# Residuals that lie in the output and are added onto by transfers, and last products by column halves, at the end of a diffusion trunk layer

## The chip, the cores and the metric

One core of a Trainium2 chip. The metric is the device time of one execution in microseconds (us). A profiled execution gives the trace; its times count from the start of its span.

## What is computed

One trunk layer for 128 context tokens and 512 latent tokens, 1024 wide: a mixer of attention and a gated convolution, then a feed-forward part, each normalised and added back with a gate.

```
mo, k, v = mixer(u, p, rope_tabs, ctx_k, ctx_v)
h = h + g1 * rms_norm(mo, p["g_post1"])
u = rms_norm(h, p["g_pre2"]) * (1 + sc2) + sh2
h = h + g2 * rms_norm(conv_ffn(u, p), p["g_post2"])

def conv_ffn(u, p):
    up = dwconv3(u @ p["w_up"], p["conv_ffn"])
    g, val = jnp.split(up, 2, axis=-1)
    return (jax.nn.silu(g) * val) @ p["w_down"]
```

The change concerns the last line of the layer: the product with w_down (2816 x 1024), the root of its mean square, the gain g_post2 * gate, and the addition of h, the residual of the mixer's half.

## The kernel before

The 640 tokens are five tiles of 128, t = 0 (context) and 1 to 4 (latent). The matrices are float32, and each product is made of three: high by high, high by low, low by high part (`mm3`, lines 235 to 237 of the trace's program).

**The stage of w_o** (near 617 to 645 us). For each tile `residual(t)` makes h on VectorE (DVE) in a buffer WR, and SyncE (SP) stores it to a scratch in HBM, hd[t] (line 1732). The normalised h goes on into w_up.

**The stage of w_down** (from about 940 us on). The activations come back from HBM in pairs of 128 rows. The first 512 output columns of every tile are finished near 1000 us: `first_half(t, pm)` squares them on ScalarE (ACT) with a running sum, multiplies them by the gains on DVE into EX[:, t, 0:512], adds the epsilon, and has SP load hd[t] into HX[:, t, :] (line 2341). EX holds five tiles of 1024 columns; it is what is stored in the end.

The last 512 columns follow. For the latent tiles the 2 x 2 blocks of tokens and columns are put together from seven products, `part(p, n)`, with sums on DVE in the buffers RAWS and A. The context tile has plain products, `context(p)`, into a PSUM bank pms[0]: for each pair p two k-steps of three products of 512 columns. The order of the work is the order in which the code is written; the three last pairs (`held`) are ordered so that the blocks finish one after another: tiles 3 and 4 first, then 1 and 2, then the context tile, whose 18 products are TensorE's last work.

What happens to a tile when its block is complete:
- `second_half(t, src)` (from line 2346): ACT squares the second 512 columns with a running sum. For latent tiles POOL adds both sums (line 2355) and raises the result to the power -1/2 (line 2356). For the context tile ACT takes a square root (2352) and DVE a reciprocal (2353), and DVE multiplies the PSUM bank by the gains (2351).
- `scaled2(t, x)` (line 2361): DVE multiplies the second halves of two tiles by the gains into EX.
- `stored(t, n)` (lines 2366 to 2369): in n pieces, DVE makes EX * root + HX, and SP stores the piece to the rows `yrows(t)` of the output. Tile 3 goes in one piece, the others in halves.

```
    def stored(t, n=1):
        r = ssqs[:, t, 1:2]
        for i in range(n):
            cs = slice(i * D // n, (i + 1) * D // n)
            V.scalar_tensor_tensor(out=EX[:, t, cs], in0=EX[:, t, cs], scalar=r, in1=room["h"][:, t, cs], op0=ALU.mult, op1=ALU.add)
            nc.sync.dma_start(yrows(t)[:, cs], EX[:, t, cs])
```

Each engine works through its own queue in order; waits are on counters of the other engines and of the DMA queues. SP issues every transfer of this stretch, in the order of the code. `ssqs[:, t, :]` holds the running sums and then the root of tile t. At the very end SP waits for the landing of all transfers and the engines meet in a barrier (line 2521).

Of the kernel before, what the change touches and what calls it, by code (L numbers as in the profile page):

```python
# [12 lines left out]
F32 = mybir.dt.float32  # L13
# [4 lines left out]
AF = mybir.ActivationFunctionType  # L18
ALU = mybir.AluOpType
# [6 lines left out]
NT = 5  # L26
# [8 lines left out]
NACT = NCOL - 2  # L35
PARTS = (((0, 128, 1), (128, 320, 130)), ((0, 320, 322),))
NRING = 4
FLAG = 3
DLAG = 4
EPS = 1e-6  # L40
O_K, O_V, O_B, O_C, O_X, O_GA, O_GC = 1024, 1280, 1536, 2560, 3584, 4608, 5632
# [71 lines left out]
def trunk_layer(ctx, tc, x_prompt, x_sample, cache_k, cache_v, c, c_ctx, w_ada, b_ada, g_pre1, g_post1, g_pre2,  # L113
                g_post2, w_in, q_norm, k_norm, w_att_out, conv_w, w_conv_out, w_o, w_up, conv_ffn, w_down, rope,
                y_prompt, y_sample, new_k, new_v):
    nc = tc.nc
    V, S, G, PE = nc.vector, nc.scalar, nc.gpsimd, nc.tensor
# [10 lines left out]
    def yrows(t):  # L128
        return y_prompt if t == 0 else y_sample[(t - 1) * 128:t * 128, :]
# [18 lines left out]
    def region(pool, tag, shape, dtype, name):  # L148
        return pool.tile([128] + shape, dtype, tag=tag, name=name)
# [20 lines left out]
    def ps1():  # L170
        turn[1] += 1
        return psa.tile([128, 512], F32, tag=f"s1{turn[1] % 2}", name=nm("s1"), bufs=1)
# [7 lines left out]
    state = {"next": 0, "raw": [], "cut": [], "limit": 10}  # L180
# [77 lines left out]
    mhalf = const.tile([128, 8], F32, name="mhalf")  # L258
# [13 lines left out]
    hd = dp.tile([NT, 128, D], F32, name="hd")  # L272
# [101 lines left out]
    with tc.tile_pool(name="pro", bufs=2) as pro, tc.manual_schedule(engines={mybir.EngineType.SP}):  # L374
# [258 lines left out]
        for f in range(2, KT):  # L633
# [32 lines left out]
            if f == KT - 3:  # L666
                V.tensor_scalar(out=gains[0], in0=gains[0], scalar1=HD ** -0.5, scalar2=None, op0=ALU.mult)
                for i in range(2):
                    for a in range(2):
                        V.tensor_tensor(out=tabs[i][:, :, 0, a * 32:a * 32 + 32], in0=rt[:, :, 0, a * 32:a * 32 + 32],  # L670
                                        in1=gains[i][:, :, a * 32:a * 32 + 32].broadcast_to((128, 4, 32)), op=ALU.mult)
                        for hf in range(2):
                            d0, s0 = a * 32 + hf * 16, a * 32 + (1 - hf) * 16
                            V.tensor_tensor(out=tabs[i][:, :, 1, d0:d0 + 16], in0=rt[:, :, 1, d0:d0 + 16],
                                            in1=gains[i][:, :, s0:s0 + 16].broadcast_to((128, 4, 16)), op=ALU.mult)
            if f == KT - 2:
                cut_upto(9)
                p = ps1()
# [11 lines left out]
    AH = Halves(NTOK, F32R, "AH")  # L690
    AL = region(ra, "r3", [KT, NTOK], F32R, "AL")
# [55 lines left out]
    with tc.tile_pool(name="att", bufs=1) as at:  # L747
# [11 lines left out]
        ssqs = at.tile([128, 4, 4], F32, name="ssqs")  # L759
# [13 lines left out]
        held = {}  # L773
# [126 lines left out]
        for t in range(NT):  # L900
# [30 lines left out]
            h = work(f"k{t} hi", "ACT", k_hi, [tk], [pk])  # L931
# [121 lines left out]
        for n, (g, t, pi) in enumerate(steps):  # L1053
# [52 lines left out]
            else:  # L1106
                pts[n], exs = [], []
                for h in hs:
# [16 lines left out]
                    if h:  # L1125
# [3 lines left out]
                                                                                   accum_out=mk[:, 4 + h:5 + h]), [mx], [ar[h]] + [er] * way)  # L1129
# [43 lines left out]
            if pi in (None, 1):  # L1173
                u = vcol[:, 2 * g + (t > 0):2 * g + (t > 0) + 1]
# [19 lines left out]
                r = work(f"R{n}", "ACT", spread, list(pvs), [pvr, xr])  # L1194
                o = work(f"O{n}", "DVE", whole, [r], [pvr, xr])
                a = work(f"AH{n}", "ACT", ah, [o], [pvr])
# [45 lines left out]
    sm_ = ctx.enter_context(tc.tile_pool(name="sm", bufs=2))  # L1242
# [11 lines left out]
    cut, raws, pair, TT = {}, {}, {}, {}  # L1254
# [474 lines left out]
    def residual(t):  # L1729
        h = WR[:, 2 + t % 3, :]  # L1730
        V.scalar_tensor_tensor(out=h, in0=TX[:, 2 + t % 2, :], scalar=roots[t], in1=h, op0=ALU.mult, op1=ALU.add)
        nc.sync.dma_start(hd[t], h)

    def sq_h(t):
        S.activation(TX[:, 4, :], WR[:, 2 + t % 3, :], AF.Square, accum_out=ssq[t][:, 2:3])
# [32 lines left out]
    room = {}  # L1768
# [115 lines left out]
    def wd_step(pm, t, act, w, start, stop):  # L1884
        c0 = 0 if t == 0 else 1 + t * 128
        mm3(pm, act[0][:, c0:c0 + 128], act[1][:, c0:c0 + 128], *w, start, stop)
# [16 lines left out]
    def second_gate(j):  # L1903
        i = j - DLAG
        accs = [[room["c+"], room["s"][:, 4, :]], [room["raw"][:, 4, :]]]
# [7 lines left out]
    def second_gate_load(j):  # L1913
        i = j - DLAG
        if i == 2 * KT:
# [6 lines left out]
    def strassen(j):  # L1922

        f, nxt = j - FLAG, j + 1 if j + 1 < NJ else None
        g = NJ - FLAG if nxt is None else None
        cg, cv = crows(j)
# [54 lines left out]
        if nxt:  # L1981
# [54 lines left out]
    for q in range(4):  # L2036
# [11 lines left out]
        elif q == 1:  # L2048
            half_load(0)
            p = bank(6)  # L2050
# [18 lines left out]
        for t in range(NT):  # L2069
# [5 lines left out]
            if q == 3 and t == 2:  # L2075
                p = bank(7)
# [142 lines left out]
    NPAIR, NP0 = NJ // 2 - 2, 1  # L2219
    A0 = region(ra, "r0", [4, 2 * NACT], F32R, "A0")  # L2220
    A1 = region(ra, "r1", [4, 2 * NACT], F32R, "A1")
    AL, AH = [A0[:, i, :] for i in range(3)], [A0[:, 3, :], A1[:, 0, :], A1[:, 1, :]]
# [3 lines left out]
    EX = region(rb, "r4", [NT, D], F32, "EX")  # L2226
    GJ = rb.tile([128, 2560], F32, tag="r5a", name="GJ")
    G2, JK = GJ[:, 0:2048].rearrange("p (r c) -> p r c", r=2), GJ[:, 2048:2560]
    RAWS = rb.tile([128, 2560], F32, tag="r5b", name="RAWS")
    SR, TR, C22 = RAWS[:, 0:1024], RAWS[:, 1024:2048], RAWS[:, 2048:2560]  # L2230
    SS, TS = {}, {2: T2}
    ssqs = sm_.tile([128, NT, 2], F32, name="ssqs", bufs=1)

    def s_room(p):
        i = p % 3
# [93 lines left out]
    def context(p):  # L2329
        u = state["cut"][base + p]  # L2330
        for k in range(2):
            a = [x[p % 3][:, k * NACT:(k + 1) * NACT] for x in (AH, AL)]
            wd_step(pms[0], 0, a, u.at(k), False, p == NPAIR - 1 and k == 1)

    def first_half(t, pm):
        row = 1 if t == 0 else 0
        first = ssqs[:, t, 0:1]
        S.activation(JK, pm, AF.Square, accum_out=first)
        V.tensor_tensor(out=EX[:, t, 0:512], in0=pm, in1=G2[:, row, 0:512], op=ALU.mult)
        V.tensor_scalar(out=first, in0=first, scalar1=D * EPS, scalar2=None, op0=ALU.add)  # L2340
        nc.sync.dma_start(room["h"][:, t, :], hd[t])

    def halves_of(x):
        return x.rearrange("p (i c) -> p i c", i=2)

    def second_half(t, src):
        row = 1 if t == 0 else 0
        first, second = ssqs[:, t, 0:1], ssqs[:, t, 1:2]
        S.activation(halves_of(JK), src, AF.Square, accum_out=second)  # L2349
        if t == 0:  # L2350
            V.tensor_tensor(out=EX[:, t, 512:1024], in0=pms[0], in1=G2[:, row, 512:1024], op=ALU.mult)
            S.activation(second, second, AF.Sqrt, bias=first)
            V.reciprocal(second, second)
        else:
            G.tensor_tensor(out=second, in0=second, in1=first, op=ALU.add)  # L2355
            G.tensor_tensor(out=second, in0=second, in1=mhalf[:, 0:1], op=ALU.pow)

    def scaled2(t, x):
        for i in range(2):
# [3 lines left out]

    def stored(t, n=1):
        r = ssqs[:, t, 1:2]
        for i in range(n):
            cs = slice(i * D // n, (i + 1) * D // n)
            V.scalar_tensor_tensor(out=EX[:, t, cs], in0=EX[:, t, cs], scalar=r, in1=room["h"][:, t, cs], op0=ALU.mult, op1=ALU.add)
            nc.sync.dma_start(yrows(t)[:, cs], EX[:, t, cs])


    pms = [bank(b) for b in RING if b not in BANKS[NJ - 1]] + [bank(BANKS[NJ - 1][1])]
# [19 lines left out]
    w, x, y = NJ - 3, NJ - 2, NJ - 1  # L2392
# [30 lines left out]
    base = state["next"]  # L2423
# [34 lines left out]
    held = range(NPAIR - HELD, NPAIR)  # L2458
# [20 lines left out]
    for p in held:  # L2479
        part(p, 2)  # L2480
    V.tensor_tensor(out=C1[:, 0, :], in0=accs[2], in1=p1, op=ALU.add)
    stored(3)
    for p in held:
        part(p, 3)
    V.tensor_tensor(out=C1[:, 1, :], in0=accs[3], in1=u4, op=ALU.add)
    for t in (1, 2):
        second_half(t, C1[:, :, (t - 1) * 256:t * 256])
    scaled2(1, C1)
    for p in held:
        context(p)  # L2490
    for t in (4, 1, 2):
        stored(t, 2)
    second_half(0, halves_of(pms[0]))
    stored(0, 2)
    fixed.close()

# [28 lines left out]
```

## Time and profile before

| what | value |
|---|---|
| median of 3 runs | 1074.96 us (1074.27 to 1075.36) |
| profiled execution, its own time | 1074.79 us |
| its span (first to last instruction) | 1073.0 us |
| granted TensorE clock | 0.999 |
| busy: PE / DVE / ACT / POOL | 1056.8 / 899.9 / 598.4 / 133.1 us |
| read from and written to HBM | 123.31 MB / 17.36 MB |

The span is 1.8 us shorter than the execution's own time. PE is TensorE's products, PEld its weight loads, SPq the queue of SP. A line such as L2368 is a line of the program before. In rows of the timeline the first number is the start, the second the length; in square brackets stands the idle time before it and what ended it.

### The profile page before, as it was taken

What the parts mean: (1) busy time and instruction counts of PE and PEld (TensorE: products, weight loads), DVE (VectorE), ACT (ScalarE), POOL (GpSimd) and SP (SyncE); (2) the same over time, 40 slices, a digit from 0 to 9 for tenths busy, and PEclk for the clock granted to TensorE, in tenths of its full rate; (3) what the DMA queues carried; (4) which work ended last, traced back from release to release, by engine and by line L of the source; (5) the groups of instructions that cost most, each with busy time, mean ns of one, the idle gap of its engine ahead of it and who ended that gap; (6) DMA issues with size and microseconds to landing.
All of it is one profiled execution on the core that took longest, in us unless ns stands there. A gap on an engine that the chain in (4) does not pass through costs nothing.

```text
span 1073.0 us, 20652 instructions
## 1 busy us (share of the span) xinstructions
PE 1056.8 (98%) x8216; PEld 995.4 (93%) x8216; DVE 899.9 (84%) x1379; ACT 598.4 (56%) x1057; POOL 133.1 (12%) x162
## 2 busy tenths in 40 slices
PE   8999999999999999999999999999999999999997
PEld 6788898899999999999998789999999999999996
DVE  5699999865498999896599678889999988989897
ACT  5478999942344544445322366645555555546673
POOL 1087676500000000000000020000000000000001
PEclk9999999999999999999999999999999999999999
DMA  9829999962244333223668634434544534436873
GB/s 320 256 82 175 190 168 187 191 147 60 75 123 124 93 103 94 79 79 99 189 188 253 198 131 129 121 116 136 166 131 152 150 122 131 152 116 219 277 275 115
DMA packets 243197, 164.02 MB, mean 153 GB/s; under 512 B 94874, under 2 KB 216214, under 8 KB 243102
## 3 DMA queue, kind: packets, MB, share of 16 engines
q1 hardware_dynamic: 242990, 162.68, 55.5%
q8 instruction: 64, 1.05, 0.4%
q14 instruction: 31, 0.25, 0.1%
q10 hardware_dynamic: 112, 0.04, 0.0%
HBM read 123.31 MB, written 17.36 MB: 131 GB/s over the span
## 4 chain that ended last, share of the span: by engine, by line
PE 90%; DVE 3%; ACT 2%; DMA 1%; POOL 1%; issue 1%; SPq 1%; DVEq 0%; ACTq 0%; POOLq 0%
PE b L1274 47%; PE b L235 10%; PE b L237 10%; PE b L236 9%; PE s L709 4%; PE s L1073 2%; PE s L1170 2%; PE s L235 1%; PE s L237 1%; PE s L1162 1%; PE s L478 1%; DVE marks L1120 1%; PE s L236 1%; PE b L1900 1%; ACT P L1134 1%
## 5 line engine op out<-in xcount | busy, mean ns | idle before, releaser
L1274 PE MATMUL b<-ZBr,whi 128*128 128x320 f32 x688 | 152.1, 309 | 0.0
L1274 PE MATMUL b<-MT,whi 128*128 128x320 f32 x608 | 134.4, 309 | 0.0
L1274 PEld LDWEIGHTS b<-ZBr,whi 128*128 128x128 f32 x688 | 114.9, 188 | 0.1
L1274 PE MATMUL b<-ZBr,wlo 128*128 128x320 f32 x344 | 106.1, 308 | 0.0
L1274 PEld LDWEIGHTS b<-MT,whi 128*128 128x128 f32 x608 | 101.7, 188 | 0.0
L1274 PE MATMUL b<-MT,wlo 128*128 128x320 f32 x304 | 94.0, 309 | 0.0
L1261 ACT ACTIVATE whi<-SUM 128x1024 fp32r<-128x1024 f32 x40 | 42.2, 1055 | 78.3 <-DVE SUM L1813 75.7
L1843 DVE SCALAR_TENSOR_TENSOR Y<-C,cffn,Y 128x642 f32<-128x642 f32 x88 | 77.9, 886 | 0.9
L1261 ACT ACTIVATE whi<-WB 128x1024 fp32r<-128x1024 f32 x38 | 40.2, 1058 | 55.5 <-DVE WB L1368 55.5
L1274 PE MATMUL b<-ZBT,whi 128*128 128x320 f32 x320 | 71.0, 308 | 0.0
L1274 PE MATMUL b<-UL,whi 128*128 128x320 f32 x228 | 70.8, 311 | 0.0
L1274 PE MATMUL b<-UH,wlo 128*128 128x320 f32 x228 | 70.1, 307 | 0.0
L1274 PE MATMUL b<-UH,whi 128*128 128x320 f32 x228 | 69.7, 306 | 0.0
L1282 ACT ACTIVATE p<-b 128x320 f32<-128x320 f32 x78 | 34.1, 437 | 55.3 <-PE b L1274 53.5
L1274 PEld LDWEIGHTS b<-ZBr,wlo 128*128 128x128 f32 x344 | 64.6, 188 | 0.0
L1265 DVE TENSOR_TENSOR wlo<-raw,whi 128x1024 fp32r<-128x1024 f32 (+1 forms) x51 | 50.4, 1020 | 13.4 <-ACT whi L1261 13.4
L1274 PEld LDWEIGHTS b<-MT,wlo 128*128 128x128 f32 x304 | 57.1, 188 | 0.0
L1274 PEld LDWEIGHTS b<-ZBT,whi 128*128 128x128 f32 x320 | 54.2, 188 | 1.6
L1120 DVE TENSOR_REDUCE marks<-s 128x1 f32<-128x640 f32 x64 | 52.1, 817 | 4.0 <-PE s L1073 3.8
L1265 DVE TENSOR_TENSOR wlo<-WB,whi 128x1024 fp32r<-128x1024 f32 x38 | 46.5, 1224 | 8.8 <-ACT whi L1261 8.7
L2355 POOL TENSOR_TENSOR ssqs<-ssqs 128x1 f32<-128x1 f32 x4 | 1.4, 356 | 412.9 <-ACT GJ L2349 412.9
L1261 ACT ACTIVATE whi<-raw 128x1024 fp32r<-128x1024 f32 (+1 forms) x51 | 43.5, 892 | 15.4 <-DMA raw<-in_w_o_dram 12.5
(477 smaller groups left out, 3348.1 us busy)
## 6 DMA issues: line engine op xcount, KB each, us to landing
raw<-in_w_in_dram SPq DMA_DIRECT2D x48, 512.0 KB
RAW<-in_w_up_dram SPq DMA_DIRECT2D x40, 512.0 KB
raw<-in_w_down_dram SPq DMA_DIRECT2D x22, 512.0 KB
GA<-in_w_ada_dram SPq DMA_DIRECT2D x16, 512.0 KB
actd<-Y SPq DMA_DIRECT2D x18, 321.0 KB
actl<-ACTb SPq DMA_DIRECT2D x18, 321.0 KB
A<-actl SPq DMA_DIRECT2D x9, 642.0 KB
A<-actd SPq DMA_DIRECT2D x9, 642.0 KB
```

The source lines that it names most:

```text
L235: PE.matmul(out, ah, bh, start=start, stop=False)
L236: PE.matmul(out, ah, bl, start=False, stop=False)
L237: PE.matmul(out, al, bh, start=False, stop=stop)
L709: PE.matmul(out, a, b, start=start and n == 0, stop=stop and n == 2, skip_group_check=True)
L1073: PE.matmul(o[h], q_of(hl, i, rows), kk[kx][rows, g, ks], start=m == 0, stop=m == 2, tile_position=(64 * h, 0), skip_group_check=True)
L1120: V.tensor_reduce(out=mk[:, h:h + 1], in_=s_of(), axis=AX.X, op=ALU.max, negate=True)
L1170: PE.matmul(p[64 * h:64 * h + 64, i * 128:i * 128 + 128], VH[:, w, s, vc_], src, start=k == 0 and m == 0, stop=k == ks[-1][0] and m == 2, ...
L1261: S.activation(to[0], raw, AF.Copy)
L1265: V.tensor_tensor(out=lo, in0=raw, in1=hi.bitcast(F32), op=ALU.subtract)
L1274: PE.matmul(out, p[:, ws], q[:, k, :], start=start and k == 0 and n == 0, stop=stop and k == 3 and n == 2, skip_group_check=True)
L1282: S.activation(t, pair[j][b], AF.Copy)
L1843: V.scalar_tensor_tensor(out=y, in0=crows(j)[i][:, d:d + NACT], scalar=cffn[:, 44 * d + o:44 * d + o + 1], in1=y, op0=ALU.mult, op1=ALU.add)
```

## The change

Three edits, all for the end of the kernel.

1. Tiles 3 and 4 (`ADDED`) no longer use the scratch: in the stage of w_o their residual is stored straight into the output's rows, and is not loaded into HX later. At the end ACT multiplies the tile in EX by its root, 1024 columns in one pass, and POOL issues a transfer that adds EX onto the output's rows. Tile 4 moves ahead, beside tile 3.
2. The context tile's last pair (`context_end`) does its products by column halves: first both k-steps for columns 0 to 255, then both for 256 to 511; twelve products of 256 columns in place of six of 512.
3. The context tile's squares are taken in two pieces of 256 columns (`context_half`), with a third running sum; POOL adds the first of them to the sum of the first half.

```
+ADDED = (3, 4)
...
     def residual(t):
...
-        nc.sync.dma_start(hd[t], h)
+        nc.sync.dma_start(yrows(t) if t in ADDED else hd[t], h)
...
-    ssqs = sm_.tile([128, NT, 2], F32, name="ssqs", bufs=1)
+    ssqs = sm_.tile([128, NT, 3], F32, name="ssqs", bufs=1)
...
-            wd_step(pms[0], 0, a, u.at(k), False, p == NPAIR - 1 and k == 1)
+            wd_step(pms[0], 0, a, u.at(k), False, False)
+
+    def context_end(p):
+        u = state["cut"][base + p]
+        for c in (0, 256):
+            for k in range(2):
+                a = [x[p % 3][:, k * NACT:(k + 1) * NACT] for x in (AH, AL)]
+                wd_step(pms[0][:, c:c + 256], 0, a, u.at(k, c, 256), False, c > 0 and k == 1)
...
     def first_half(t, pm):
...
-        nc.sync.dma_start(room["h"][:, t, :], hd[t])
+        if t not in ADDED:
+            nc.sync.dma_start(room["h"][:, t, :], hd[t])
...
     def second_half(t, src):
...
         S.activation(halves_of(JK), src, AF.Square, accum_out=second)
-        if t == 0:
-            V.tensor_tensor(out=EX[:, t, 512:1024], in0=pms[0], in1=G2[:, row, 512:1024], op=ALU.mult)
+        G.tensor_tensor(out=second, in0=second, in1=first, op=ALU.add)
+        G.tensor_tensor(out=second, in0=second, in1=mhalf[:, 0:1], op=ALU.pow)
+
+    def context_half(i):
+        first, second, third = (ssqs[:, 0, k:k + 1] for k in range(3))
+        src = pms[0][:, i * 256:i * 256 + 256]
+        S.activation(JK[:, i * 256:i * 256 + 256], src, AF.Square, accum_out=(third, second)[i])
+        if i == 0:
+            G.tensor_tensor(out=first, in0=first, in1=third, op=ALU.add)
+        else:
+            V.tensor_tensor(out=EX[:, 0, 512:1024], in0=pms[0], in1=G2[:, 1, 512:1024], op=ALU.mult)
             S.activation(second, second, AF.Sqrt, bias=first)
             V.reciprocal(second, second)
...
     def stored(t, n=1):
         r = ssqs[:, t, 1:2]
+        if t in ADDED:
+            S.activation(EX[:, t, :], EX[:, t, :], AF.Copy, scale=r)
+            G.dma_start(yrows(t), EX[:, t, :], accum_op=ALU.add)
+            return
...
     stored(3)
+    stored(4)
...
     scaled2(1, C1)
-    for p in held:
+    for p in held[:-1]:
         context(p)
-    for t in (4, 1, 2):
+    context_end(held[-1])
+    for t in (1, 2):
         stored(t, 2)
-    second_half(0, halves_of(pms[0]))
+    for i in range(2):
+        context_half(i)
     stored(0, 2)
```

In the orders below, the counter names in square brackets are the engines that an instruction waits for; ssqs are the running sums and roots, mhalf a constant -1/2.

POOL at the end of w_down, before (tiles 3, 4, 1, 2 in turn, a sum and a power each):

```order
L2355 TENSOR_TENSOR ssqs<-ssqs 128x1 [waits Activation_49]
L2356 TENSOR_TENSOR ssqs<-ssqs,mhalf 128x1 [waits Pool_49]
L2355 TENSOR_TENSOR ssqs<-ssqs 128x1 [waits DVE_49,Activation_49]
L2356 TENSOR_TENSOR ssqs<-ssqs,mhalf 128x1 [waits Pool_49]
L2355 TENSOR_TENSOR ssqs<-ssqs 128x1 [waits Activation_49]
L2356 TENSOR_TENSOR ssqs<-ssqs,mhalf 128x1 [waits Pool_49]
```

and POOL there now, from tile 4's sum on:

```order
L2358 TENSOR_TENSOR ssqs<-ssqs 128x1 [waits DVE_49,Activation_49]
L2359 TENSOR_TENSOR ssqs<-ssqs,mhalf 128x1 [waits Pool_49]
L2382 DMA out_dram<-EX 128x1024 [waits Activation_49] x2
L2358 TENSOR_TENSOR ssqs<-ssqs 128x1 [waits Activation_49]
L2359 TENSOR_TENSOR ssqs<-ssqs,mhalf 128x1 [waits Pool_49]
L2366 TENSOR_TENSOR ssqs<-ssqs 128x1 [waits Activation_49]
```

The two adding transfers stand between tile 4's power and tile 1's sum, and wait for ACT's passes; the context tile's extra sum comes last.

ACT at the end of w_down, before (b is the context tile's PSUM bank, RAWS the finished latent blocks):

```order
L2349 ACTIVATE GJ,ssqs<-RAWS 128x512 [waits DVE_49,Activation_49]
L2349 ACTIVATE GJ,ssqs<-RAWS 128x512 [waits Activation_49]
L2349 ACTIVATE GJ,ssqs<-b_877_11090 128x512 [waits PE_49,Activation_49]
L2352 ACTIVATE ssqs<-ssqs 128x1 [waits Activation_49]
L2521 UNCONDITIONAL_BRANCH
```

and ACT there now:

```order
L2381 ACTIVATE EX<-EX,ssqs 128x1024 [waits DVE_49,Pool_49]
L2381 ACTIVATE EX<-EX,ssqs 128x1024 [waits Pool_49]
L2357 ACTIVATE GJ,ssqs<-RAWS 128x512 [waits DVE_49,Activation_49]
L2357 ACTIVATE GJ,ssqs<-RAWS 128x512 [waits Activation_49]
L2364 ACTIVATE GJ,ssqs<-b_877_11090 128x256 [waits PE_49,Activation_49]
L2364 ACTIVATE GJ,ssqs<-b_877_11090 128x256
L2369 ACTIVATE ssqs<-ssqs 128x1 [waits Activation_49,Pool_49]
```

The two passes over tiles 3 and 4 stand ahead of the squares of tiles 1 and 2; of the two squares of the context tile only the first waits for PE, and the square root now waits for POOL as well.

On DVE the combinations of tiles 3 and 4 (one of 1024 columns, two of 512) are gone; the rest stands as it did.

More of the change, by code (lines that the diff above doesn't have):

```diff
@@ L2346, in second_half @@
     def second_half(t, src):
-        row = 1 if t == 0 else 0
         first, second = ssqs[:, t, 0:1], ssqs[:, t, 1:2]
         S.activation(halves_of(JK), src, AF.Square, accum_out=second)
-        if t == 0:
-            V.tensor_tensor(out=EX[:, t, 512:1024], in0=pms[0], in1=G2[:, row, 512:1024], op=ALU.mult)
+        G.tensor_tensor(out=second, in0=second, in1=first, op=ALU.add)
[8 more added lines that the diff above has]
+            V.tensor_tensor(out=EX[:, 0, 512:1024], in0=pms[0], in1=G2[:, 1, 512:1024], op=ALU.mult)
             S.activation(second, second, AF.Sqrt, bias=first)
             V.reciprocal(second, second)
-        else:
-            G.tensor_tensor(out=second, in0=second, in1=first, op=ALU.add)
-            G.tensor_tensor(out=second, in0=second, in1=mhalf[:, 0:1], op=ALU.pow)
     def scaled2(t, x):
```

## The prediction

> **What bounds the kernel now.** The page comes first: where the chain that ended last spends its time.
>
> ```profile
> span 1073.0 us, 20652 instructions
> ...
> PE 90%; DVE 3%; ACT 2%; DMA 1%; POOL 1%; issue 1%; SPq 1%; DVEq 0%; ACTq 0%; POOLq 0%
> ```
>
> TensorE carries the chain. The busy time by stretches says whether anything ahead of the last products can gain or lose; the columns are the length, then busy time (instructions) of PE, PEld, DVE, ACT and POOL, the clock, the DMA share and GB/s.
>
> ```profile
> core 0: us, PE busy (x) PEld busy (x) DVE busy (x) ACT busy (x) POOL busy (x), PEclk, DMA share, GB/s
> 617.00:650.00 33.00, 33.00 (x189) 28.98 (x188) 23.63 (x37) 22.96 (x50) 8.77 (x21) 1.00 0.37 130
> 994.40:1000.00 5.60, 5.60 (x30) 4.54 (x29) 4.66 (x9) 4.38 (x10) 0.00 (x0) 1.00 0.84 272
> 979.00:1061.60 82.60, 82.60 (x592) 77.54 (x591) 76.19 (x113) 51.68 (x65) 2.36 (x4) 1.00 0.59 205
> ```
>
> PE is busy in every microsecond of these, so work that is taken from the DMA engines there lies under products. What is left is the tail; the chain in order of time (start, length, what):
>
> ```profile
> 1061.66 0.13 PE b L237
> 1061.80 0.02 issue
> 1061.82 0.69 DVE RAWS L2485
> 1062.52 1.20 DVE EX L2361 x2
> 1063.71 1.14 DVE EX L2368 x2
> 1064.86 0.10 issue
> 1064.95 2.73 DVE EX L2368 x4
> 1067.69 0.60 DVE EX L2351
> 1068.29 0.08 DVE ssqs L2353
> 1068.39 0.75 DVE EX L2368
> ```
>
> From 1061.8 on the chain is DVE's: products finished at 1061.8, then tile 4's two halves, four halves of tiles 1 and 2, and tile 0. PE itself runs on until about 1066. After DVE come the last stores, so the DMA engines in the tail belong to the picture:
>
> ```profile
> 1062.40:1063.80 1.40, 1.40 (x8) 1.13 (x7) 1.40 (x4) 1.16 (x3) 0.35 (x1) 1.00 0.92 375
> 1063.80:1065.20 1.40, 1.40 (x8) 1.13 (x7) 1.40 (x3) 0.29 (x2) 1.28 (x3) 1.00 0.00 0
> 1065.20:1069.40 4.20, 0.75 (x4) 0.28 (x2) 4.17 (x8) 0.98 (x3) 0.91 (x1) 1.00 1.00 374
> 1069.40:1070.00 0.60, 0.00 (x0) 0.00 (x0) 0.41 (x1) 0.00 (x0) 0.00 (x0) 1.00 0.03 7
> 1070.00:1071.40 1.40, 0.00 (x0) 0.00 (x0) 0.00 (x0) 0.00 (x0) 0.00 (x0) 0.88 0.99 372
> 1071.40:1073.00 1.60, 0.00 (x0) 0.00 (x0) 0.00 (x0) 0.00 (x0) 0.00 (x0) 0.50 0.01 3
> ```
>
> This is the table I argue from. Between 1062.4 and 1071.4 the 16 engines carry the five output tiles in 1.40 x 0.92 + 4.20 + 0.60 x 0.03 + 1.40 x 0.99 = 6.90 us, 1.38 us a tile of 512 KB, and stand idle for 9.0 - 6.9 = 2.1 us. They were full for 4.2 us at a stretch. Shortening DVE's chain helps only as far as these engines have room, and the change gives them more to do.
>
> **The change part by part.** Stage of w_o: two stores go to the output's rows instead of the scratch, the same bytes from the same queue: 0. Behind it two loads of the scratch fall away from SP's queue near 995; PE was full there (5.60 of 5.60): 0, and nothing shown waits in its place.
>
> DVE loses tile 3's combination (1.28 us) and tile 4's (the 1.14 us at 1063.71). What is late next? POOL's root for tile 1:
>
> ```profile
> 1060.22 0.19 POOL L2355 TENSOR_TENSOR ssqs<-ssqs 128x1 f32<-128x1 f32 x1
> 1060.49 1.49 POOL L2356 TENSOR_TENSOR ssqs<-ssqs,mhalf 128x1 f32<-128x1 f32 x1
> 1059.71 0.55 POOL L2356 TENSOR_TENSOR ssqs<-ssqs,mhalf 128x1 f32<-128x1 f32 x1
> 1063.41 0.35 POOL L2355 TENSOR_TENSOR ssqs<-ssqs 128x1 f32<-128x1 f32 x1 [1.43 <-ACT GJ L2349]
> 1067.61 0.68 DVE L2351 TENSOR_TENSOR EX<-b,GJ 128x512 f32<-128x512 f32 x1
> L2356 POOL TENSOR_TENSOR ssqs<-ssqs,mhalf 128x1 f32<-128x1 f32 x4 | 3.9, 980 | 0.3
> ```
>
> The power takes 0.55 us beside a DVE that reads PSUM and 1.49 beside the combination, which is gone now. From the sum at 1063.41 it is 0.27 (1060.22 to 1060.49) + 0.55 + about 0.1 to DVE: tile 1 can start at 1064.35 instead of 1064.95, and four halves (2.66 us, 1064.95 to 1067.61) end at 1067.0.
>
> ACT gets two passes of 128x1024. They must not delay the squares of tile 1, which began at 1062.61.
>
> ```profile
> 1043.58 1.04 ACT L2258 ACTIVATE SS<-RAWS 128x1024 fp32r<-128x1024 f32 x1
> 1062.61 0.63 ACT L2349 ACTIVATE GJ<-RAWS 128x512 f32<-128x512 f32 x1 [2.85 <-DVE RAWS L2485]
> 1066.05 0.60 ACT L2349 ACTIVATE GJ<-b 128x512 f32<-128x512 f32 x1 [1.96 <-PE b L237]
> 1066.54 0.19 ACT L2349 ACTIVATION_READ_ACCUMULATOR GJ<-b 128x1 f32 x1
> 1066.77 0.29 ACT L2352 ACTIVATE ssqs<-ssqs 128x1 f32<-128x1 f32 x1
> ```
>
> Tile 3's root is there at 1060.26, so the passes run from 1060.3 to 1061.35 and on to 1062.4, inside the 2.85 us in which ACT idled: 0, cover 0.2 us.
>
> Column halves. In the order of ACT the second half-square has no wait on PE of its own, so the first one's wait already covers the last product: nothing starts earlier. PE pays nothing: a product of 512 columns takes 0.23 us and one of 256 takes 0.12 (rows below), twelve for six. ACT pays: 512 columns more cost 1.04 - 0.63 = 0.41 us, so 256 fewer save 0.21 of the 0.49 between 1066.05 and 1066.54. Two halves with their reads are 2 x (0.28 + 0.23) = 1.02 against 0.72; bounds are half of 0.49 and all of it, 0.96 to 1.44. The squares end at 1067.07, and DVE's product for tile 0, queued behind a wait for both, begins at 1067.1 instead of 1067.61. POOL's extra sum for tile 0 lies under the second half-square. **DVE's chain is 0.5 us shorter.**
>
> ```profile
> 1042.30 0.23 PE b L237
> 1061.43 0.12 PE b L235
> ```
>
> The issue on POOL is not in the trace. Bounds: 0.33 us, as SP issues, and 1.49, POOL's longest instruction of the stretch; I take POOL's mean, 0.98. The first leaves POOL at 1061.35 + 0.98 = 1062.35, the second at 1062.4 + 0.98 = 1063.4, just when the sum for tile 1 (1063.41), queued behind both, is due. Under the Trainium skill, "DMA: Bandwidth & Descriptors", section on latency and other measured facts, the first byte of a DMA generated in software comes after about 1 us against 0.6 in hardware; the sum would be the same by it, and no run here shows it yet.
>
> The transfers themselves. SP's issue at 1061.61 lasts 0.35 us and the engines fill at 1062.4, 0.44 later.
>
> ```profile
> 1061.61 0.35 SPq L2369 DMA_DIRECT2D out_dram<-EX  x1
> 1069.84 0.33 SPq L2369 DMA_DIRECT2D out_dram<-EX  x1
> ```
>
> So an adding transfer begins at 1062.35 + 0.44 = 1062.8. Its price is the open question: at least a plain store, 1.38 us; it must also read the old row, as the removed load did, so 2.76; and nothing excludes more (three passes, 4.14). I take 2.76, the load and the store that it replaces. Then the engines need 2 x 2.76 + 3 x 1.38 = 9.66 us from 1062.8, without a gap, since each transfer is ready before its turn (the last half, issued at 1069.84 before, half a microsecond earlier: 1069.3 + 0.33 + 0.44 = 1070.1): they end at **1072.5 instead of 1071.4**. The 2.1 us of idle time is used up, and DVE's 0.5 is lost in the queue. The 1.6 us behind (landing, SP's wait, barrier) stay. **Sum: +1.0 us**, 1074.79 to 1075.8 in the profiled execution; the median lies 0.17 higher: 1076.0.
>
> In the Trainium skill, "Collectives: The Full Stack", section "The bandwidth ceiling", a reducing transfer runs at half a copy's rate because it needs two source reads on one ring, not because of the add. By that rule the sum is the same 2.76; by the lower bound it would be DVE's -0.5. The trace has no such transfer to agree or not.
>
> **The rivals.** The forecast decides wherever an adding transfer costs over 2.23 us: 1062.8 + 2a + 4.14 = 1071.4.
> - *The read is hidden* (a below 2.0). DVE's side sets the end: -0.5, 1074.5. For it: a stretch of mostly loads, the row below, moves 403 GB/s, more than the stores' 374, so reading is not what sets a store's rate. Against: a share of 1.00 leaves no free time in the engines beside a plain store.
>
> ```profile
> 1000.00:1004.00 4.00, 4.00 (x33) 3.90 (x32) 4.00 (x12) 1.92 (x4) 0.00 (x0) 1.00 1.01 403
> ```
>
> - *An adding transfer costs three passes or more*: slower. 1062.8 + 2 x 4.14 + 4.14 = 1075.2, +3.8: 1078.8. It is over the 0.2% from a = 3.3 us. For it: nothing here shows such a unit's rate; against: whole rows of 4 KB, as the plain stores.
> - *POOL's issue is long*, the first one after none at all in this kernel. With X us each, the engines end at 1061.35 + X + 0.44 + 9.66, +0.05 + X against before; roots of tiles 1 and 2 wait as well but are later only from X = 2.7. X = 2.5 gives +2.55: 1077.5. POOL's first sum after a long idle took 0.54 us where the next took 0.19 (above), so a first issue can well be slow.
>
> ```profile
> 1059.09 0.54 POOL L2355 TENSOR_TENSOR ssqs<-ssqs 128x1 f32<-128x1 f32 x1 [411.48 <-ACT GJ L2349]
> ```
>
> - *The halves do what they say*, if the first square starts with half of the products undone: 0.5 us earlier on ACT, and DVE is then bound by tiles 1 and 2 at 1067.0: 0.1 us, hidden under the transfers: 1076.0 all the same.
>
> **How the numbers follow.** Forecast 0.45, read hidden 0.22, three passes 0.18, long issue 0.10, halves 0.05. A measurement of this kernel can tell about 0.2%, 2.15 us, from no change. Slower by that: the three passes, half of the long issue and a small tail of the forecast, 0.26; faster has no path that I can price (DVE's side ends at -0.5), 0.02 for what I overlook; the rest, 0.72, is within. The range reaches from the hidden read with a cheap issue, 1074.3, to three passes, 1078.8. The forecast's own range is 1075 to 1077.
>
> **What would show it.** Right: no gap in the DMA share from 1062.8 to about 1072.5, DVE's last combination ending near 1069.3, POOL issues near 1 us, and a later landing of the last DMA. Wrong: a DMA share that falls to zero before the last store (the read was hidden), a share of 1.00 beyond 1074 (more passes), or POOL's sum for tile 1 well after 1063.4. If ACT's first half-square starts before PE's last product, the step on the halves is wrong. If PE idles before 1061, my zeros for the earlier stages are.

## The result and the profile after

| | median | runs | lowest to highest |
|---|---|---|---|
| before | 1075.16 us | 6 | 1074.27 to 1076.23 |
| after | 1079.51 us | 6 | 1077.81 to 1082.53 |

The change is slower: ratio 1.0046, 95% interval 1.0036 to 1.0056. Predicted were 1076.0 and no change that can be told. Further down the same kernel runs twice more beside other runs of before, at 1.0027 (1.0016 to 1.0039) and 1.0030 (1.0020 to 1.0039): still slower, but nearer 3.3 us than 4.35.

The profiled execution took 1081.47 us, with this span:

```profile
core 0: 1079.5 us, clock 0.996
```

The last product, of before and of after, shows where its 6.5 us more of span lie.

```profile
1065.56 0.39 PE L237 MATMUL b<-whi,A 128*128 128x512 f32 x1
```

```profile
1069.20 0.27 PE L238 MATMUL b<-whi,A 128*128 128x256 f32 x1
```

TensorE is done at 1069.47, where before it was 1065.95: 3.52 us are lost ahead of the tail, 2.98 in it (10.03 us from there to the end, 7.05 before).

**Ahead of the tail.** The sign of being wrong that was named last, a PE that idles before 1061, came true. Busy time in 44 us of the attention, of after, with the columns as in the prediction's windows:

```profile
196.00:240.00 44.00, 41.04 (x520) 38.15 (x519) 27.22 (x50) 28.36 (x58) 7.40 (x6) 0.96 0.82 158
```

and of before:

```profile
196.00:240.00 44.00, 43.01 (x544) 40.42 (x543) 30.43 (x52) 29.35 (x59) 7.39 (x6) 1.00 0.86 168
```

PE's longest wait there, in after (us in all, times, longest):

```profile
PE s L1171 <- DMA PT<-P: 2.4, 1, 2.4
```

A transpose by DMA came late, and behind it the granted clock fell to 0.66 between 208 and 212 us. The next long run of products on the chain, of before and of after, shows the whole 3.52 us (289.96 - 286.44):

```profile
286.44 134.97 PE b L1274 x924
```

```profile
289.96 134.95 PE b L1275 x924
```

So all of it is lost before 290 us; the distance is the same at the end. The nearest edit is some 370 us later than the wait (the stage of w_o). Whether the loss belongs to the change, the other runs below have to tell.

**The tail.** To compare with before, take 3.52 off each time of after. POOL and ACT, after (start, length, what, idle time before it and what ended it):

```profile
1065.26 2.00 POOL L2382 DMA_DIRECT2D out_dram<-EX  x2 [0.72 <-ACT EX L2381]
1066.91 0.58 POOL L2358 TENSOR_TENSOR ssqs<-ssqs 128x1 f32<-128x1 f32 x1
1067.57 0.56 POOL L2359 TENSOR_TENSOR ssqs<-ssqs,mhalf 128x1 f32<-128x1 f32 x1
```

```profile
1063.79 2.19 ACT L2381 ACTIVATE EX<-EX,ssqs 128x1024 f32<-128x1024 f32 x2 [0.53 <-POOL ssqs L2359]
1069.57 0.38 ACT L2364 ACTIVATE GJ<-b 128x256 f32<-128x256 f32 x1 [1.99 <-PE b L238]
1069.94 0.38 ACT L2364 ACTIVATE GJ<-b 128x256 f32<-128x256 f32 x1
```

SP's store issues, the passes and POOL's issues one by one (ns, min/median/max), after:

```profile
L2387 SPq DMA_DIRECT2D out_dram<-EX x6: 351/918/1182, 1068.9 to 1073.9; - x6
...
L2381 ACT ACTIVATE EX<-EX,ssqs x2: 1138/1145/1152, 1063.8 to 1064.8; 128x1024 f32<-128x1024 f32 x2
L2382 POOL DMA_DIRECT2D out_dram<-EX x2: 977/1036/1095, 1065.3 to 1066.3; - x2
```

The two passes lie in ACT's old idle time, the issues of the adding transfers take 1.0 us each, and the sum for tile 1 comes at 1063.39, where 1063.41 was foretold. The first half-square begins behind PE's last product. DVE:

```profile
1068.16 2.74 DVE L2386 SCALAR_TENSOR_TENSOR EX<-EX,ssqs,HX 128x512 f32<-128x512 f32 x4 [0.96 <-POOL ssqs L2359]
1070.82 0.68 DVE L2368 TENSOR_TENSOR EX<-b,GJ 128x512 f32<-128x512 f32 x1
1071.61 1.42 DVE L2386 SCALAR_TENSOR_TENSOR EX<-EX,ssqs,HX 128x512 f32<-128x512 f32 x2
```

DVE ends at 1073.03, less 3.52 is 1069.51, 0.30 us earlier than before (1069.81). So up to here the tail is a little shorter, and it is still 3 us longer at the end. The windows of the DMA engines, of after, have the rest (the last two columns are their share and GB/s):

```profile
1066.40:1067.20 0.80, 0.80 (x6) 0.62 (x5) 0.80 (x2) 0.77 (x3) 0.80 (x2) 1.00 1.22 82
1067.20:1068.00 0.80, 0.80 (x5) 0.67 (x4) 0.00 (x1) 0.38 (x2) 0.72 (x3) 1.00 0.39 56
1068.00:1068.80 0.80, 0.80 (x9) 0.80 (x8) 0.64 (x1) 0.00 (x0) 0.72 (x3) 1.00 0.89 169
...
1071.20:1072.00 0.80, 0.00 (x0) 0.00 (x0) 0.76 (x3) 0.00 (x0) 0.00 (x0) 1.00 0.88 177
...
1075.20:1076.00 0.80, 0.00 (x0) 0.00 (x0) 0.00 (x0) 0.00 (x0) 0.00 (x0) 0.50 1.06 407
1076.00:1076.80 0.80, 0.00 (x0) 0.00 (x0) 0.00 (x0) 0.00 (x0) 0.00 (x0) 0.50 0.89 343
1076.80:1077.60 0.80, 0.00 (x0) 0.00 (x0) 0.00 (x0) 0.00 (x0) 0.00 (x0) 0.50 0.20 74
1077.60:1078.40 0.80, 0.00 (x0) 0.00 (x0) 0.00 (x0) 0.00 (x0) 0.00 (x0) 0.50 0.05 18
```

Three things are to be seen. While the adding transfers run, a full share moves some 180 GB/s; with plain stores alone it moves 407. At the start little is moved (56 GB/s). The share of 0.39 there is not idle time: a window counts the whole time of a packet where the packet starts, and the first ones, which started in the window above (share 1.22), are long. And the end is ragged: from 1076.8 on, a fifth of the engines' time and then a twentieth is still busy. What the packets of each queue took from 1055 to 1085 (30 us), POOL's queue first: number of packets, MB, and their time as a share of the 16 engines' time; the last line is POOL's two issues, with the us from issue to landing.

```profile
q0 software_dynamic: 288, 1.05, 21.1%
q1 hardware_dynamic: 864, 1.57, 13.7%
...
out_dram<-EX POOLq DMA_DIRECT2D x2, 512.0 KB, 7.3
```

Two adding tiles took 0.211 x 30 = 6.33 us, 3.17 each; three plain ones 4.11, 1.37 each. SP's waits for landings at the very end, after (us in all, times, longest):

```profile
SPq L2542 <- DMA out_dram<-EX: 3.6, 5, 1.2
```

and before:

```profile
SPq L2521 <- DMA out_dram<-EX: 1.7, 2, 1.0
```

### The profile page after: what moved, and what is told of

Read it like the earlier page. It is cut to its first block, busy times and chain, and to the rows that moved or that the text cites. A ratio compares the mean times of both kernels' runs of the same rounds, so it can differ in the third digit from the quotient of the medians.

```text
span 1079.5 us, 20662 instructions
## 1 busy us (share of the span) xinstructions
PE 1058.6 (98%) x8222; PEld 997.3 (92%) x8222; DVE 897.5 (83%) x1376; ACT 601.7 (56%) x1061; POOL 134.2 (12%) x165
## 4 chain that ended last, share of the span: by engine, by line
PE 90%; DVE 2%; ACT 2%; POOL 2%; DMA 2%; issue 1%; SPq 1%; DVEq 0%; POOLq 0%; ACTq 0%
PE b L1275 47%; PE b L236 10%; PE b L238 10%; PE b L237 10%; PE s L710 4%; PE s L1074 2%; PE s L1171 2%; PE s L236 1%; PE s L1163 1%; PE s L238 1%; PE s L479 1%; POOL wlo L832 1%; PE s L237 1%; PE b L1901 1%; DMA araw<-in_w_ada_dram 1%
## 5 line engine op out<-in xcount | busy, mean ns | idle before, releaser
L1262 ACT ACTIVATE whi<-SUM 128x1024 fp32r<-128x1024 f32 x40 | 42.2, 1055 | 78.2 <-DVE SUM L1814 75.7
```

The lines of the kernel that those rows point to most:

```text
L1262: S.activation(to[0], raw, AF.Copy)
```

## The experiments

Theory: the adding transfers make the whole loss in the tail. Rivals: the halves cost it; POOL's queue is dear, not the addition; the stage near 200 us is slowed by the change, or by chance. "Tail" is the time from the end of PE's last product to the end of the span; "above before" compares medians of one chip.

**Halves alone.**

```
-ADDED = (3, 4)
+ADDED = ()
...
-    for t in (1, 2):
+    for t in (4, 1, 2):
         stored(t, 2)
```

> The context tile's products and squares by column halves as in the change, but no adding transfers: tiles 3 and 4 are combined on DVE and stored by SP as before. Theory (the adding transfers and POOL's software queue make the whole loss: about 3.0 us in the tail, and 0 to 4.6 us near 200 us, where the transposes of attention run): 0 to -0.2 us, 1075, the two half-squares hidden under DVE's stores; first half-square starts only after PE's last product. Rival A (the halves cost): +1 us or more. Rival B (the loss near 200 us is chance and comes with any kernel): runs scatter up to +4 us here too.

1075.31 us (12 runs) against 1074.92 (35 runs): 1.0001 (0.9993 to 1.0009). Tail 6.96. Without adding transfers the halves cost nothing and bring nothing: PE's last product, then ACT's first half-square of this kernel.

```profile
1066.37 0.27 PE L238 MATMUL b<-whi,A 128*128 128x256 f32 x1
```

```profile
1066.74 0.38 ACT L2364 ACTIVATE GJ<-b 128x256 f32<-128x256 f32 x1 [1.99 <-PE b L238]
```

**Adding transfers alone**, the context tile's products and squares whole.

```
-    context_end(held[-1])
+    context(held[-1])
...
-    for i in range(2):
-        context_half(i)
+    context_whole()
```

> The adding transfers as in the change, but the context tile's products and squares whole, as before. Theory: the same loss as the change, +3 us in the tail, total +3 to +5 us with a wide scatter between runs. Rival A (the halves cost): near before, within 1 us.

1077.26 us (12 runs): 1.0020 (1.0010 to 1.0031), 2.3 above before. Tail 9.03, and the packets nearly as in the change:

```profile
q0 software_dynamic: 288, 1.05, 20.8%
```

The adding transfers, then, though with 2.0 us of tail and not the 3 expected. This end is sharp, and so 1 us earlier than that of the change:

```profile
1072.00:1072.80 0.80, 0.00 (x0) 0.00 (x0) 0.00 (x0) 0.00 (x0) 0.00 (x0) 0.50 1.05 405
1072.80:1073.60 0.80, 0.00 (x0) 0.00 (x0) 0.00 (x0) 0.00 (x0) 0.00 (x0) 0.50 0.36 136
1073.60:1074.40 0.80, 0.00 (x0) 0.00 (x0) 0.00 (x0) 0.00 (x0) 0.00 (x0) 0.50 0.00 0
```

**POOL's transfers without the addition**, and **the same stores from SP**. Both leave out the residual of tiles 3 and 4 at the end.

```
-            G.dma_start(yrows(t), EX[:, t, :], accum_op=ALU.add)
+            G.dma_start(yrows(t), EX[:, t, :])
```

> The change with POOL's two transfers as plain stores: the residual of tiles 3 and 4 is left out of the sum. Theory: a plain store costs 1.4 us of the engines instead of 3.2, so the engines end about 3.5 us earlier than in the change and the tail is that of before or 0.3 us shorter; what the software queue does near 200 us stays, +0 to +4 us, scattered. Rival C (it is the queue that POOL issues on, not the addition, that makes the transfers dear): the software queue's share stays at about 3 us a tile and the tail at +3 us. Rival B: no loss near 200 us beyond that of before.

> The change with the two transfers as plain stores from SP: the residual of tiles 3 and 4 is left out of the sum, POOL issues nothing. Theory: tail -0.3 us (DVE's chain is shorter and the engines have room), and no loss near 200 us: 1074.8, scatter as before. Rival B (chance near 200 us): scatter up to +4 us as in the change. If the loss near 200 us shows here, the queue is not its cause but something else in the change (the shifted counters of the DMA queues, the larger tile of sums).

1074.60 (0.9995, 0.9987 to 1.0004) and 1075.09 (1.0000, 0.9990 to 1.0010), 12 runs each; both tails 6.31. From POOL without the addition:

```profile
q0 software_dynamic: 288, 1.05, 8.8%
```

That is 0.088 x 30 = 2.64 us for two tiles, 1.32 each, like SP's. POOL's queue is not dear; the addition is. The two kernels also show what the relief of DVE is worth when nothing is paid for it: 7.05 - 6.31 = 0.74 us of the tail (0.3 was expected), which is below what the medians can tell.

**One adding transfer, and four**, on top of the kernel without halves.

```
-ADDED = (3, 4)
+ADDED = (3,)
```

> Adding transfers alone, but for tile 3 only; tile 4 is combined on VectorE and stored by SP at its old place. Theory (the price goes by the tile: 3.12 us of the engines for an adding tile, 1.37 for a plain one): the engines need 3.12 + 4 x 1.37 = 8.6 us from 1062.6, or 1071.2 without a gap, where before they ended at 1071.4; with the gap of 0.5 to 0.8 us seen behind the first adding transfer's start, 1071.7 to 1072.0: median 1075.0 to 1075.6. Rival F (a fixed cost of having an adding transfer in flight at all, since SP's stores stand behind it, whatever the number): about that of two, 1076.8 to 1077.3.

> Adding transfers alone, for tiles 1 to 4; only the context tile is combined on VectorE and stored by SP. Theory (price by the tile): the engines need 4 x 3.12 + 1.37 = 13.85 us against 10.35 with two adding tiles, 3.5 more: median near 1080.8 (1080.0 to 1082), the adding transfers' queue taking 6.2 us x 2 = 12.5 us of the engines' time. Rival F (fixed cost): 1076.8 to 1077.8. Rival S (several adding transfers at once slow each other down, so that the price grows with their number): 1082 and above, with a price of a tile over 3.5.

One: 1075.81 (1.0013, 1.0004 to 1.0022; 11 runs), 1.4 above before, between the theory's range and rival F's. Four, with `ADDED = (1, 2, 3, 4)`: 1081.13 (1.0066, 1.0049 to 1.0083; 6 runs), 6.7 above, as the theory has it. The adding queue's packets in 30 us, with one:

```profile
q0 software_dynamic: 144, 0.52, 11.5%
```

and with four, where the steady stretch is long enough to read its rate:

```profile
q0 software_dynamic: 576, 2.10, 38.2%
```

```profile
1070.00:1071.00 1.00, 0.00 (x0) 0.00 (x0) 0.00 (x0) 0.00 (x0) 0.00 (x0) 0.50 1.05 209
```

One takes 3.45 us and four take 11.46 (12.5 were expected): (11.46 - 3.45) / 3 = **2.67 us for each and 0.78 once**. These are packet times of one execution each; that with four was the fastest of its six (1079.17 us, tail 11.77). Two would take 6.12 by that; the profiles have 6.15 to 6.78. The fixed cost (rival F) alone falls, since four cost far more than two. A growing price (rival S) falls too: four take 2.87 each, one 3.45. Steadily, an adding transfer moves 209 GB/s where plain stores move 407, a ratio of 0.51. The half rate that the Trainium skill gives for a reduction in "Collectives: The Full Stack", section "The bandwidth ceiling", agrees with this.

**VectorE relieved in another way.** The kernel before, with tile 4 scaled by ACT, its residual added by POOL, and stored by SP.

```
+        if t == 4:
+            S.activation(EX[:, t, :], EX[:, t, :], AF.Copy, scale=r)
+            G.tensor_tensor(out=EX[:, t, :], in0=EX[:, t, :], in1=room["h"][:, t, :], op=ALU.add)
+            nc.sync.dma_start(yrows(t), EX[:, t, :])
+            return
...
-    for t in (4, 1, 2):
+    for t in (1, 2, 4):
```

> The kernel before, with no adding transfer and no halves, but tile 4 is taken off VectorE's chain in another way: ScalarE multiplies it by its inverse root (1.04 us in its idle time from 1064.1), GpSimd adds the residual (not in any row so far), SP stores it behind tiles 1 and 2. Theory (what the plain transfers showed, 0.5 us of VectorE's chain, can be had without the addition by transfer): the chain ends 0.5 us earlier, median about 1074.4. Rival P (GpSimd's addition takes over 2.2 us, or slows VectorE beside it): the chain or tile 4's store ends later than before, 1075.0 to 1076.5.

1077.28 (1.0027, 1.0018 to 1.0036; 10 runs), 2.9 above before: rival P, and more than its range. POOL and DVE:

```profile
1065.37 2.48 POOL L2368 TENSOR_TENSOR EX<-EX,HX 128x1024 f32<-128x1024 f32 x1
```

```profile
1064.23 4.83 DVE L2373 SCALAR_TENSOR_TENSOR EX<-EX,ssqs,HX 128x512 f32<-128x512 f32 x4 [0.71 <-POOL ssqs L2356]
```

DVE's four halves take 4.83 us beside POOL's addition; in the change they took 2.74. So 2.1 us are lost on DVE for 2.48 on POOL.

**The change again, twice**, the second time beside **the adding transfers alone, again**, and **the halves with one adding transfer**. The first three have no edit that has not been shown; the last is the change with `ADDED = (3,)` and tile 4 back at its old place.

> The changed kernel itself, for the second time and beside other runs of the kernel before. Its first runs lay 4.35 us above the kernel before, the kernel with the adding transfers alone only 2.3 us. Theory (the adding transfers make the tail about 2 us longer, the rest of the first runs' loss lay in the wait for attention's transposes near 200 us, which comes and goes by chance): median about 1077.3 (1076.7 to 1078.0), tail from TensorE's last product to the end of the span near 9.0, no wait of 2.4 us at the transposes in most executions. Rival H (halves and adding transfers together cost what neither does alone): median 1078.7 or more again, with a tail near 10.0 and a ragged end of the transfers. Rival U (the change does something to the stages near 200 us): TensorE's last product again over 2 us later than before.

> The changed kernel once more, now beside the adding transfers alone on the same chip. Its profiles so far ended raggedly, some engines of the transfers 1 us and more behind the others. Theory (the halves do nothing, and a ragged end is a matter of the execution): the median lies within 0.5 us of the adding transfers alone, both 2.3 to 3.3 above the kernel before. Rival H (halves and adding transfers together cost about 1 us more than the adding transfers alone): 0.8 us or more above them.

> The adding transfers alone (products and squares of the context tile whole), again. Theory: within 0.5 us of the changed kernel, 2.3 to 3.3 us above the kernel before. Rival H: 0.8 us or more below the changed kernel, with an end of the transfers that is not ragged.

> The halves with one adding transfer (tile 3), tile 4 stored plainly at its old place. With one adding transfer and no halves the median lay 1.4 us above the kernel before. Theory (halves do nothing): 1.1 to 1.7 above. Rival H (the two together cost about 1 us more): 2.2 or more above.

The change: 1077.72 (6 runs) and 1077.75 (10 runs), 3.3 and 3.2 above before. Adding transfers alone: 1076.85 (1.0021, 1.0013 to 1.0030; 11 runs), 2.3 above again. Halves with one: 1076.02 (1.0008, 1.0000 to 1.0017; 11 runs), 1.5 above, as without halves. Neither new profile of the change has a wait of more than 0.6 us in the attention, and TensorE ends at 1066.00 and 1065.80 (before: 1065.95), so rival U falls. This execution of the adding transfers alone has the wait, again 2.4 us; its clock stays at 1.00 there, and TensorE ends 2.0 us later than before and not 3.5.

But on one chip the change lay 0.9 above the adding transfers alone, by the expectations rival H's side (0.8 or more), and the change's tails were 10.2 and 9.4 here, this one's 8.99. With one adding transfer H fails, with two it was alive.

**Which half?** Products alone by halves, squares alone by halves, and the change with the sum of the two half squares moved from POOL to DVE.

```
-            G.tensor_tensor(out=first, in0=first, in1=third, op=ALU.add)
+            V.tensor_tensor(out=first, in0=first, in1=third, op=ALU.add)
```

> The adding transfers and the products of the context tile by column halves, its squares whole. Theory (halves do nothing): 2.3 to 2.8 us above the kernel before, as the adding transfers alone (2.3 and 2.3), and a sharp end of the transfers. Rival H in the products: 3.1 or more above, with a ragged end.

> The adding transfers and the squares of the context tile by column halves (GpSimd adds the two sums), its products whole. Theory (halves do nothing): 2.3 to 2.8 us above the kernel before. Rival H in the squares, or in GpSimd's small addition while its transfers are under way: 3.1 or more above, with a ragged end.

> The changed kernel with one instruction moved: VectorE, not GpSimd, adds the two half sums of squares (0.19 us on GpSimd). Theory: no effect beyond 0.3 us against the changed kernel (3.2 and 3.3 above the kernel before). Rival G (GpSimd's addition at 1066.65 hinders the software queue's transfers that are still under way): 2.3 to 2.6 above the kernel before, as without the halves.

Products: 1079.07 (1.0038, 1.0026 to 1.0051; 5 runs), 4.5 above. Squares: 1078.46 (1.0033, 1.0024 to 1.0042; 11 runs), 3.9 above. Sum on DVE: 1077.82 (1.0029, 1.0017 to 1.0041; 6 runs), 3.3 above, so rival G falls. By the expectations the first two are rival H's. But each half alone comes out worse than both together (3.3, on the same chip), and two costs that add up can't do that.

**A neutral edit, and the worst kernel again.** The first is the adding transfers alone with one idle instruction more; the second is the products by halves.

```
+    S.activation(ssqs[:, 0, 2:3], mhalf[:, 0:1], AF.Square)
     scaled2(1, C1)
```

> The adding transfers alone with one idle instruction more: a square of one column that nothing reads, on ScalarE in its idle time behind the squares of tiles 1 and 2. It has no half. Theory D (the price of two adding transfers varies between programs and executions by 1 us or more, and the halves have no part in it): it may lie anywhere from 2.3 to 4.5 us above the kernel before, and its time goes with the time that the adding queue's packets take. Rival H (the halves cost it): 2.3 us above, as twice before, with a sharp end.

> The adding transfers with the products alone by halves, again: 4.5 us above the kernel before in the first runs. Theory D: anywhere from 2.3 to 4.5. Rival H (the halved products cost 1 us or more of the tail): 3.2 or more again, with a ragged end.

Neutral edit: 1077.71 (1.0027, 1.0018 to 1.0036; 11 runs), 2.9 above. Products again: 1077.94 (1.0029, 1.0018 to 1.0041; 6 runs), 3.2 above where it was 4.5, which is within D's range and at the edge of H's. The kernel with no half now has the ragged end as well:

```profile
1073.60:1074.40 0.80, 0.00 (x0) 0.00 (x0) 0.00 (x0) 0.00 (x0) 0.00 (x0) 0.50 0.66 251
1074.40:1075.20 0.80, 0.00 (x0) 0.00 (x0) 0.00 (x0) 0.00 (x0) 0.00 (x0) 0.50 0.20 77
1075.20:1076.00 0.80, 0.00 (x0) 0.00 (x0) 0.00 (x0) 0.00 (x0) 0.00 (x0) 0.50 0.15 56
```

So a ragged end needs no half. The trace's list of packets shows what it goes with. An adding packet of 4 KB takes 0.33 us at the median; in most of these executions one or three of them, always near the start of the second adding transfer (among the 131st to 160th of 256), take 1.62 to 2.29 us. The engines that carry them end late: the share of 0.20 above is that of about three engines of 16, and its packets are SP's plain ones, in three series side by side. All ten profiles with two adding transfers, from the lowest share of q0 in 30 us:

| kernel | q0 | adding packets over 1.5 us | tail, us |
|---|---|---|---|
| adding alone, second | 20.5% | none | 8.99 |
| products by halves, second | 20.5% | 1.62 | 9.74 |
| adding alone, first | 20.8% | none | 9.03 |
| the change, second | 20.9% | 1.80 | 10.20 |
| products by halves, first | 21.1% | 1.93 | 9.99 |
| the change, first | 21.1% | 1.91 | 10.03 |
| the change, third | 21.2% | none | 9.40 |
| adding alone, neutral edit | 21.4% | 2.05, 2.13, 2.26 | 10.49 |
| sum on DVE | 21.5% | 2.11, 2.18, 2.29 | 10.48 |
| squares by halves | 22.6% | 2.15, 2.26, 2.28 | 10.70 |

They have 1.9 to 3.7 us more tail than before, 2.9 on the mean. The tail goes with these packets better than with the share: 8.99 to 9.40 with none, 9.74 to 10.20 with one, 10.48 to 10.70 with three. The change itself stands among those with none and those with one, the kernel without halves among those with none and those with three. No packet over 1.5 us stands in the profiles with one or with four adding transfers, nor in POOL's plain ones.

## Why the prediction was wrong

**The step that failed** is the sum's end of the transfers: "they end at 1072.5 instead of 1071.4", and "the 1.6 us behind stay", +1.0. The price of a tile in it was right. The sum started the transfers too early, gave their first packets no cost of their own, and took the 16 engines to end together, a term put at nothing. With the change's own 3.52 us taken off, the windows and the list of packets put it so:

- *Price of a tile*, 2.76 foretold: the slope is 2.67. What the sum lacked is the 0.78 us that adding costs once. Most of it lies in the first packet of each engine: in after these 16 took 0.97 us on the mean, the other adding packets 0.36. The price was read off plain transfers in a full queue; nothing in before's trace showed a start.
- *The start*, 1062.8 foretold: POOL's first issue began 0.33 us after ACT's pass (1063.79 + 1.14 = 1064.93, then 1065.26), a hand-over that I had not counted, and lasted 1.10 us, not 0.98. The window up to 1066.8 is empty; the first packet starts at 1066.92, less 3.52 that is 1063.4, 0.6 us later.

```profile
1066.60:1066.80 0.20, 0.20 (x3) 0.15 (x2) 0.20 (x2) 0.20 (x2) 0.20 (x1) 1.00 0.00 0
```

- *The even end.* From 1076.0 on the shares still hold (0.89 + 0.20 + 0.05) x 0.8 = 0.91 us, so evenly spread work would end at 1076.9, less 3.52 is 1073.4: 0.9 later than foretold, 0.6 of it the start. The work itself took 1073.4 - 1063.4 = 10.0 us where 9.66 were foretold. (The packet times add up to more, 6.33 + 4.11 = 10.44, since packets overlap where a share stands above 1.00.)
- *The engines don't end together.* The last one works until 1078.2, 1.3 us longer. One adding packet, from 1070.13 on, took 1.91 us, and the share of 0.05 at the end is about that of one engine of 16. From there to the end of the span it is 1.3 us (1.6 foretold).

Together 0.9 + 1.3 - 0.3 = 1.9, which with the +1.0 of the forecast makes the tail's +2.98 but for rounding. In the two sharpest ends the first part stands alone: 1.0 + 0.9 = 1.9, and they have 1.94 and 1.98 more tail than before. The forecast's mechanism (the engines are the bound and take back what DVE gains) was right, the size was a third of it. Beside the 4.35 us of the first six runs there are the 3.3 of the later ones: by those the time would lie inside the range given, and still outside the forecast's own 1075 to 1077.

**The zeros ahead of the tail** hold as far as the runs tell: the 2.4 us wait stands in one execution each of two kernels and in none of the other two of the change. Both have adding transfers, as 13 of the 18 profiles have, so that these make the wait more frequent is not excluded. Of 123 runs of the kernel before on these chips four lay above 1077 us, up to 1079.46. That those had this same wait is not shown, since none of them was profiled. Why the first six runs of the change lay 1 us above its later ones is open; the profiled one of them had the wait, the others have no trace.

**DVE's 0.5 us** came to 0.30 in the change, since POOL's sum for tile 1, right behind the two issues, and the step to the power took 0.66 us (1066.91 to 1067.57), not 0.27: tile 1 started at 1064.64 (1068.16 - 3.52), not 1064.35. With plain stores from SP it came to 0.54 (1068.39 + 1.42 = 1069.81 against PE's end at 1066.49 is 3.32, where before had 1069.81 - 1065.95 = 3.86). Before, and then the plain stores from SP:

```profile
1068.39 1.42 DVE L2368 SCALAR_TENSOR_TENSOR EX<-EX,ssqs,HX 128x512 f32<-128x512 f32 x2
```

```profile
1064.94 2.74 DVE L2386 SCALAR_TENSOR_TENSOR EX<-EX,ssqs,HX 128x512 f32<-128x512 f32 x4 [0.71 <-POOL ssqs L2359]
...
1068.39 1.42 DVE L2386 SCALAR_TENSOR_TENSOR EX<-EX,ssqs,HX 128x512 f32<-128x512 f32 x2
```

**ACT's passes** at no cost were right; each took 1.14 us, 0.10 more than the row used for it. **POOL's issue**, 0.98 taken, measured 0.98 and 1.10 (977 and 1095 ns): the rival of a long issue falls. **The halves** gain nothing, for the reason given: the first square starts behind the last product. Their squares took 0.83 us (1069.57 to 1070.40), cheaper than the 1.02 taken. A first half that really ends earlier was not tried.

**The rivals.** The hidden read falls (2.67 against 1.37). Three passes gave 1078.8, nearest to the first median, and a long issue 1077.5, nearest to the later two, but by a price of 4.14 and an issue of 2.5 us that no profile has. That the forecast kept only "a small tail" for over 0.2% is the second fault: a price without any row, multiplied by two and followed by an uneven end, had more ways up than down.

What stays open is why a few adding packets take 1.6 us and more in some executions, and whether the halves make them more frequent. With two adding transfers and halves the medians are 3.2 to 4.5 above before, without halves 2.3 to 2.9, and six of seven profiles with halves have such packets, one of three without. The ranges don't meet, but one program alone moved from 4.5 to 3.2, and the neutral edit has as ragged an end as any. The unprofiled runs behind the medians have no list of packets. No version here is faster than the kernel before by more than the noise.

## What to carry to other kernels

An addition by transfer is no free addition: here it took about twice the engines' time of a plain store, and 0.78 us once. By these figures it can pay only where the DMA engines have that much idle time, which the share of the windows tells (not tried here), and not behind a kernel's last products, where every transfer stands on the path, as here. When the end of a kernel is the landing of stores, reckon with the slowest of the engines, not with their mean; and before a small loss is put down to the last edit, run a neutral edit beside it.

## What the runs showed of the hardware

- Plain stores of SP hardly move beside adding ones. In after from 1065 to 1072, although SP had begun to issue four halves since 1068.9:

```profile
q0 software_dynamic: 225, 0.86, 76.6%
q1 hardware_dynamic: 3, 0.01, 0.3%
```

  The first plain packet starts 2.5 us after SP's first issue began (1068.94 to 1071.40), in before 0.8 (1061.61 to 1062.45). SP's issues were held up, too: 0.33 and 0.35 us in before (the prediction's rows), 0.92 at the median and up to 1.18 in after.

- POOL's issue of an adding transfer took 0.98 and 1.10 us in after and 0.86 to 1.09 with four; of a plain one, without the addition, 0.80, and 0.54 for the second:

```profile
1061.27 0.80 POOL L2382 DMA_DIRECT2D out_dram<-EX  x1 [0.71 <-ACT EX L2381]
1062.31 0.54 POOL L2382 DMA_DIRECT2D out_dram<-EX  x1 [0.24 <-ACT EX L2381]
```

- An adding transfer of 512 KB took 2.67 us of packet time and 0.78 once, a plain one 1.32 to 1.37; single adding packets took up to 2.29 us, 0.33 at the median.
- DVE and POOL did not add side by side: 2.48 us of POOL's addition of 128x1024 cost DVE's combinations 2.1 us.
